# Spreading 1/rms over the partitions by GpSimd's DMAs, and the order of the last row block's tail, in a transformer layer on one core

## The chip, the cores and the metric

The kernel runs on one core of one Trainium2 chip. The metric is the device time in microseconds of one execution; lower is better. The kernel before took 351.38 us, the median of three runs (351.15 to 352.08).

## The reference, cut to what matters

x has 512 tokens of width 1024. Everything is float32, and the inputs are used once.

```python
def rmsnorm(x, g):
    y = x * lax.rsqrt(jnp.mean(x * x, axis=-1, keepdims=True) + 1e-6)
    return y * g

h = rmsnorm(x, g_mix)
q_sb, k_sb, v_sb, z_sb, q_mb, k_mb, v_mb, z_mb = split(h @ w_in, 8)     # 512 columns each
o_sb = stick_breaking_attention(q_sb, k_sb, v_sb)                       # 8 heads of 64
o_mb = moba_attention(q_mb, k_mb, v_mb, alibi_slopes)                   # 8 heads of 64
y = concat([rmsnorm(o_sb, g_out_sb) * silu(z_sb), rmsnorm(o_mb, g_out_mb) * silu(z_mb)])
x = x + y @ w_out
x = x + (p @ w_ple) * sigmoid(rmsnorm(x, g_ple) @ w_ple_gate)
out = rmsnorm(x, g_final)
```

The change touches two places: the first rmsnorm, whose 1/rms multiplies the projections q, k and z after the matmul, and the last rmsnorm, for the last 128 tokens.

## The kernel before, in words

**Matmuls in three parts.** Each float32 operand is split into a high and a low part (float32r): ScalarE writes the high part (`part_hi`, L80, the instruction at L82 or L84), VectorE subtracts it (`part_lo`, L86, the instruction at L88 or L90). `mul3` (L75) is then three matmuls of 128 x 128 by 128 x 512. Weights come as units of 512 KB (`load_unit`, L160, on SyncE's queue), wait in three buffers `raw`, and are split in the order of a list (`split_unit`, L197; `pop_w`, L105, takes one high part and the low part of the one before). When the low part of a unit's second half is done, the next unit is loaded.

**The opening.** The work is written out by hand in order for TensorE (always) and for ScalarE, VectorE and GpSimd (from L60 to L587). TensorE first does p @ w_ple (`ple`), then the projections of q0 and k0, then v0 (items of the list at L147). `stream` (L440) hands out these matmuls in steps of one `mul3`, and `F0(n)` (L446) takes n steps. v0 has four weight units; TensorE goes through them for the first two token blocks together, 4 steps a unit, 16 steps in all (L393 to L400), so the last unit is wanted from the thirteenth step on.

**1/rms of x.** VectorE and ScalarE sum the squares of x, tokens on partitions (`sq_x`, L487). `find_r` (L496) makes `r4` = (mean + eps)^-0.5 by a small VectorE instruction and GpSimd's power (`rstd`, L96, power at L99). r4 has 128 partitions x 4 token blocks. The projections q, k, z come out transposed (features on partitions, tokens along the row), so they need r4 along the row on every partition: `rx`, 128 x 512. `spread_r` (L501) makes it by four TensorE transposes of r4 broadcast over columns into one bank `tp`, and one ScalarE copy (L507). `scaled` (L295, VectorE at L298) multiplies a projection by rx into `ev`; `end_q` (L304) then copies parts of ev into QH (ScalarE, L313 and L314), subtracts into QL (VectorE, L315) and clears the other half of QL (GpSimd, L312); `end_k` (L317) does much the same. v needs r4 as it is.

In the order by hand, after `find_r` come the splits of two units of v0, eight steps of TensorE (last of q0, seven of k0), `spread_r`, one more step, three `pop_w` (L566; splits of v0's later units), `end_q0` (whose first VectorE instruction is ev), the remaining splits of v0, `end_k0`, and GpSimd's `rel` (iota and affine_select). Scores of the first head follow v0's first two token blocks.

**The rest.** Sixteen heads run as a pipeline: scores on TensorE, elementwise work on ScalarE and VectorE, transposes and the sums over v, with projection steps between them. Then come the output matmul, and per block of 128 tokens the gate: matmul, sigmoid, and the final norm.

**The tail.** The last token block (t = 3, from L952) does the gate in three cuts of 512, 256 and 256 columns (`gate_cut`, L963; `end_gate`, L911), sums squares per cut (`square_sum`, L970) and scales the two halves of the output. From L982 the order on ScalarE and VectorE is written by hand. `pre` gathers the mean of the first two cuts plus eps, `r3` is (sum + pre)^-0.5 by GpSimd's power (L990). The first half ot[0] was multiplied by g_final earlier and is scaled by ScalarE (L991); the second half ot[1] is multiplied by g_final on VectorE (L989) and then scaled by r3 (L992). The halves are stored from SyncE's queue (L993) and ScalarE's queue (L994).

Of the kernel before, what the change touches and what calls it, by code (L numbers as in the profile page):

```python
# [8 lines left out]
F32 = mybir.dt.float32  # L9
# [3 lines left out]
OP = mybir.AluOpType  # L13
ET = mybir.EngineType

P = 128
S = 512
# [6 lines left out]
NT = S // P  # L24
# [10 lines left out]
def layer(ctx, tc, x, xT, pT, w_qkz, w_v, gcols, g_final, w_out, w_ple, w_gate, out):  # L35
# [12 lines left out]
    nc = tc.nc  # L48
# [8 lines left out]
    dram = ctx.enter_context(tc.tile_pool(name="dram", bufs=1, space=bass.MemoryType.DRAM))  # L57
    pp = ctx.enter_context(tc.tile_pool(name="pp", bufs=1, space=bass.MemoryType.PSUM))
# [7 lines left out]
    def bank():  # L66
        return pp.tile([P, S], F32, name="pj", bufs=2)
# [4 lines left out]
    def tr(ps, src):  # L72
        nc.tensor.transpose(ps, src, idf)  # L73
# [6 lines left out]
    def part_hi(hi, src, scale=None):  # L80
        if scale is None:
            nc.scalar.copy(hi, src)  # L82
        else:
            nc.scalar.activation(hi, src, AF.Copy, scale=scale)  # L84

    def part_lo(hi, lo, src, scale=None):  # L86
        if scale is None:
            nc.vector.tensor_sub(lo, src, hi.bitcast(F32))  # L88
        else:
            nc.vector.scalar_tensor_tensor(lo, src, scale, hi.bitcast(F32), op0=OP.mult, op1=OP.subtract)  # L90
# [5 lines left out]
    def rstd(dst, ss, n, width):  # L96
        t = sm.tile([P, NT], F32, name="rs_t")
        nc.vector.tensor_scalar(t[:, :width], ss, 1.0 / n, EPS, op0=OP.mult, op1=OP.add)
        nc.gpsimd.tensor_tensor(dst, t[:, :width], mhalf[:, :width], op=OP.pow)  # L99
# [60 lines left out]
    def load_unit():  # L160
        if n_load[0] == len(UNITS):
            return
        kind, a, u = key = UNITS[n_load[0]]
        n_load[0] += 1
        r = raws[key] = raw.tile([P, DM], F32, name="raw")
        if kind == "v":
            load(r.rearrange("p (g c) -> p g c", g=2),
                 w_v[a:a + 2, u // 2, :, u % 2 * S:(u % 2 + 1) * S].rearrange("g p c -> p g c"))
        elif kind == "o":
            half, n = a  # L170
            row = (4 * half + 2 * u) * P
            load(r.rearrange("p (k c) -> p k c", k=2),
                 w_out[row:row + 2 * P, n * S:(n + 1) * S].rearrange("(k p) c -> p k c", p=P))
        elif kind == "g":
            load(r, w_gate[a * P:(a + 1) * P, :])
        else:
            load(r, w_qkz[12 * (a // 4) + BASE[kind] + a % 4])

    def gate_tiles(k):

        if k < 2:
            if k == 0:
                wg["big"] = big.tile([P, 2, 2, DM], F32R, name="wg01", tag="hTl")
            w = wg["big"][:, k]
        elif k == 2:
            w = at.tile([P, 2, DM], F32R, name="wg2", tag="v")
        elif k == 3:
            w = wu.tile([P, 2, DM], F32R, name="wg3", tag="wu")
        else:
            tags = {4: ("QH0", "QH1", "K0", "K1"), 5: ("QH0", "QH1", "K0", "K1"), 6: ("QL0", "QL1", "QL0", "QL1"),  # L190
                    7: ("y0", "y1", "y2", "y3")}[k]
            w = [(yp if g[0] == "y" else at).tile([P, S], F32R, name=f"wg{k}{i}", tag=g)
                 for i, g in enumerate(tags)]
            return [(w[n], w[2 + n]) for n in range(2)]
        return [(w[:, 0, n * S:(n + 1) * S], w[:, 1, n * S:(n + 1) * S]) for n in range(2)]

    def split_unit():  # L197

        if n_split[0] == len(UNITS):
            return  # L200
        kind, a, u = key = UNITS[n_split[0]]
        n_split[0] += 1
        parts = []
        scale = gc[:, 2 * KT + a:2 * KT + a + 1] if kind == "g" else None

        def hi_(n):
            if not parts:
                if kind == "g":
                    wg[a] = gate_tiles(a)
                    parts.extend(wg[a])  # L210
                else:
                    w = W_[key] = wu.tile([P, 2, DM], F32R, name="wu")
                    parts.extend((w[:, 0, n * S:(n + 1) * S], w[:, 1, n * S:(n + 1) * S]) for n in range(2))
            part_hi(parts[n][0], raws[key][:, n * S:(n + 1) * S], scale)

        def lo_(n):
            part_lo(*parts[n], raws[key][:, n * S:(n + 1) * S], scale)
            if n:
                whole.add(key)
                load_unit()  # L220

        wq.extend((lambda n=n: hi_(n), lambda n=n: lo_(n)) for n in range(2))
        if n_split[0] < len(UNITS) and UNITS[n_split[0]][0] == "g":
            split_unit()
# [76 lines left out]
    rx = {}  # L301
# [116 lines left out]
    x2 = [None]  # L418
# [27 lines left out]
    def F0(n):  # L446
        for _ in range(n):
            next(fs, None)
            steps[0] += 1
# [35 lines left out]
    ss4, r4 = (cst.tile([P, NT], F32, name=n) for n in ("ss4", "r4"))  # L485

    def sq_x(t):  # L487
        x_ = xs[t // 2][:, t % 2]
        if t % 2:
            nc.vector.tensor_tensor_reduce(out=x_, in0=x_, in1=x_, scale=1.0, scalar=0.0, op0=OP.mult, op1=OP.add,  # L490
                                           accum_out=ss4[:, t:t + 1])
        else:
            junk = at.tile([P, DM], BF16, name="junk", tag="o")
            nc.scalar.activation(junk, x_, AF.Square, accum_out=ss4[:, t:t + 1])

    def find_r():  # L496

        rstd(r4, ss4, DM, NT)
        rx["t"] = r4

    def spread_r():  # L501

        ps = pp.tile([P, S], F32, name="tp", bufs=2)
        for t in range(NT):
            tr(ps[:, t * P:(t + 1) * P], r4[:, t:t + 1].broadcast_to([P, P]))
        rx["all"] = yp.tile([P, S], F32, name="rx")
        nc.scalar.copy(rx["all"], ps)  # L507

    warm(28)
    nc.vector.tensor_copy(half((0, 0))[:, 0], rh[0, 0])  # L510
# [44 lines left out]
    for t in range(NT):  # L555
        sq_x(t)
    find_r()
    split_unit()
    split_unit()
    while wq or pend:  # L560
        pop_w()
    F0(8)
    spread_r()
    F0(1)
    end_q0, end_k0 = first
    for _ in range(3):  # L566
        pop_w()
# [196 lines left out]
    for h in range(2 * NH):  # L764
        if h == 0:
            front(0)
        else:
            b = h - 1
# [47 lines left out]
    b = 2 * NH - 1  # L816
# [17 lines left out]
    gf = at.tile([P, DM], F32, name="gf", tag="B", bufs=1)  # L834
# [73 lines left out]
                 k == 0, k == KT - 1)  # L908
            tick()

    def end_gate(t, a, b, ps, r, pt, between=None):  # L911
        gs = at.tile([P, S], F32, name="tmp")
        nc.scalar.activation(gs[:, :b - a], ps[:, :b - a], AF.Sigmoid, scale=r)
        nc.vector.tensor_mul(gs[:, :b - a], gs[:, :b - a], pt)  # L914
        if between:
            between()
        nc.vector.tensor_add(x2[0][:, t, a:b], x2[0][:, t, a:b], gs[:, :b - a])  # L917

    finish((0, 0))
# [12 lines left out]
    for t in range(NT - 1):  # L932
        r = rms2(t)
        pt = [at.tile([P, S], F32, name="pl", tag="ph", bufs=2) for n in range(2)]
        for n in range(2):
            load(pt[n], pl_d[t, :, n * S:(n + 1) * S])
        for n in range(2):
            ps = bank()
# [6 lines left out]
        r3 = rms2(t)  # L945
        for n in range(2):
            ns = slice(n * S, (n + 1) * S)
            ot = at.tile([P, S], F32, name="ot", tag="plo", bufs=2)
# [3 lines left out]
    t = NT - 1  # L952
    r = rms2(t)
    pt = [at.tile([P, S], F32, name="pl", tag="ph", bufs=2) for n in range(2)]
# [3 lines left out]
    ss = sm.tile([P, 3], F32, name="ss3")  # L958
    ot = [at.tile([P, S], F32, name="ot", tag="plo", bufs=2) for _ in range(2)]
    sq = at.tile([P, S], F32, name="sq", tag="o")  # L960
    pre, r3 = (sm.tile([P, 1], F32, name=n) for n in ("pre", "r3"))

    def gate_cut(c, between=None):  # L963
        a, b = cuts[c]
        ps = bank()
        gate_steps(t, ps, range(KT), a, b)
        end_gate(t, a, b, ps, r, pt[a // S][:, a % S:a % S + b - a], between)
        return x2[0][:, t, a:b]

    def square_sum(c):  # L970
        a, b = cuts[c]
        n, xc = b - a, x2[0][:, t, a:b]
        if c:
            nc.vector.tensor_tensor_reduce(out=sq[:, :n], in0=xc, in1=xc, scale=1.0, scalar=0.0,
                                           op0=OP.mult, op1=OP.add, accum_out=ss[:, c:c + 1])
        else:
            nc.scalar.activation(sq[:, :n], xc, AF.Square, accum_out=ss[:, :1])
# [4 lines left out]
    end = tc.manual_schedule(engines={ET.Activation, ET.DVE})  # L982
    end.__enter__()
    square_sum(1)
    gate_cut(2, between=lambda: nc.vector.tensor_add(pre, ss[:, 0:1], ss[:, 1:2]))
    nc.vector.tensor_scalar(pre, pre, 1.0 / DM, EPS, op0=OP.mult, op1=OP.add)
    square_sum(2)
    nc.vector.tensor_scalar(r3, ss[:, 2:3], 1.0 / DM, pre, op0=OP.mult, op1=OP.add)
    nc.vector.tensor_mul(ot[1], x2[0][:, t, S:], gf[:, S:])  # L989
    nc.gpsimd.tensor_tensor(r3, r3, mhalf[:, :1], op=OP.pow)  # L990
    nc.scalar.activation(ot[0], ot[0], AF.Copy, scale=r3)  # L991
    nc.vector.tensor_scalar_mul(ot[1], ot[1], r3)  # L992
    nc.sync.dma_start(out[t * P:, S:], ot[1])  # L993
    nc.scalar.dma_start(out[t * P:, :S], ot[0])  # L994
    end.__exit__(None, None, None)
# [32 lines left out]
```

## Time and profile before

| | |
|---|---|
| median of 3 runs | 351.38 us (351.15 to 352.08) |
| profiled execution | 352.3 us, span 350.5 us, granted TensorE clock 0.996 |
| busy: TensorE, its weight loads | 341.8 us (98%), 285.1 us (81%) |
| busy: VectorE, ScalarE, GpSimd | 279.6 us (80%), 220.6 us (63%), 19.6 us (6%) |
| DMA | 43.31 MB, from SyncE's queue but for the last store, on ScalarE's |

The span runs from the first to the last instruction. Engines work side by side, and a busy share is an average over all stages. In the rows below PE is TensorE's matmul, PEld its weight load, DVE VectorE, ACT ScalarE, POOL GpSimd, SP SyncE; a q behind an engine's name is its instruction queue. Times are in us.

### The profile page before, as it was taken

Reading aid. Unit: us, or ns where it says so; the run is one execution under the profiler, and the core shown is the slowest. Engines: PE = TensorE matmul, PEld = TensorE weight load, DVE = VectorE, ACT = ScalarE, POOL = GpSimd, SP = SyncE. Lnnn points to the kernel's source line nnn. Section 1 sums busy time; section 2 is a strip of 40 time slices with the busy share of each in tenths; the row PEclk is TensorE's granted clock in tenths of the full one; section 3 lists DMA queues with packets and bytes.
Section 4 is the critical chain, followed back from the end, with each engine's and each line's share of the span. In section 5 each row is a group of like instructions: output and inputs, shape, how many; then the busy total and the mean of one; then the engine's idle time right before and its main releaser. Section 6 shows DMA issues by size and latency. Waiting matters only on the chain.

```text
span 350.5 us, 4873 instructions
## 1 busy us (share of the span) xinstructions
PE 341.8 (98%) x1688; PEld 285.1 (81%) x1688; DVE 279.6 (80%) x570; ACT 220.6 (63%) x416; POOL 19.6 (6%) x43
## 2 busy tenths in 40 slices
PE   8999999999999999999999999999999999999991
PEld 6788888888888888888888888888888888888891
DVE  3996799878989897989579889989899979274554
ACT  4876767664767364777387689797776753234341
POOL 2013000000000000000000100000000010000111
PEclk9999999999999999999999999999999999999998
DMA  7997815212141114111105301310911680437321
GB/s 201 422 363 236 279 25 216 75 47 66 53 144 38 65 57 152 43 55 63 52 0 180 122 1 60 122 60 4 352 65 59 184 298 29 153 90 239 122 91 60
DMA packets 17624, 43.31 MB, mean 124 GB/s; under 512 B 1856, under 2 KB 3648, under 8 KB 17600
## 3 DMA queue, kind: packets, MB, share of 16 engines
q1 hardware_dynamic: 17456, 42.75, 35.3%
q8 instruction: 13, 0.21, 0.3%
q10 hardware_dynamic: 144, 0.26, 0.2%
q14 instruction: 11, 0.09, 0.1%
HBM read 37.24 MB, written 5.77 MB: 123 GB/s over the span
## 4 chain that ended last, share of the span: by engine, by line
PE 92%; issue 2%; DMA 2%; ACT 1%; DVE 1%; SPq 0%; POOL 0%; POOLq 0%; DVEq 0%; ACTq 0%
PE pj L70 67%; PE sc L70 9%; PE av L70 8%; PE tp L73 6%; PE tp L70 3%; DMA rawh<-in_pT_dram 2%; SPq L158 0%; ACT junk L864 0%; POOL r L99 0%; POOLq L1024 0%; DVE ot L949 0%; ACT ot L991 0%; DVE tmp L914 0%; DVE x L917 0%; DVE pu L88 0%
## 5 line engine op out<-in xcount | busy, mean ns | idle before, releaser
L70 PE MATMUL pj<-hTh,wu 128*128 128x512 f32 x384 | 134.5, 401 | 0.0
L70 PEld LDWEIGHTS pj<-hTh,wu 128*128 128x128 f32 x384 | 72.2, 188 | 13.0
L70 PE MATMUL pj<-hTl,wu 128*128 128x512 f32 x192 | 75.1, 391 | 0.0
L82 ACT CAST wu<-raw 128x512 fp32r<-128x512 f32 x80 | 46.7, 618 | 24.5 <-PE pj L70 21.0
L88 DVE TENSOR_TENSOR wu<-raw,wu 128x512 fp32r<-128x512 f32 x80 | 52.8, 684 | 2.8 <-ACT wu L82 2.6
L70 PE MATMUL pj<-wg,h 128*128 128x512 f32 (+1 forms) x216 | 44.8, 368 | 0.0
L70 PEld LDWEIGHTS pj<-wg,h 128*128 128x128 f32 x216 | 37.4, 188 | 7.4
L70 PEld LDWEIGHTS pj<-hTl,wu 128*128 128x128 f32 x192 | 36.3, 189 | 5.1
L88 DVE TENSOR_TENSOR plo<-tp,ph 128x512 fp32r<-128x512 f32 (+1 forms) x48 | 28.5, 593 | 6.4 <-ACT ph L82 6.1
L82 ACT CAST ph<-tp 128x512 fp32r<-128x512 f32 (+1 forms) x48 | 24.5, 511 | 13.3 <-PE tp L73 13.2
L70 PE MATMUL pj<-wu,yh 128*128 128x512 f32 x96 | 30.9, 403 | 0.0
L70 PE MATMUL pj<-wu,hTh 128*128 128x512 f32 x96 | 30.1, 395 | 0.0
L621 DVE TENSOR_TENSOR_SCAN inc<-A,own 128x512 f32<-128x512 f32 (+3 forms) x32 | 24.7, 809 | 5.4 <-ACT A L616 5.4
L73 PEld LDWEIGHTS tp<-idf,C 128*128 128x128 f32 x160 | 20.4, 140 | 6.1
L73 PE MATMUL tp<-idf,C 128*128 128x128 f32 x160 | 25.2, 272 | 0.0
L70 PE MATMUL sc<-K,QH 128*128 128x512 f32 (+1 forms) x64 | 19.8, 323 | 0.0
L70 PEld LDWEIGHTS pj<-wu,hTh 128*128 128x128 f32 x96 | 17.3, 188 | 3.1
L658 ACT ACTIVATE C<-A,nm 128x512 f32<-128x512 f32 (+3 forms) x32 | 17.8, 558 | 3.2 <-DVE nm L654 3.0
L70 PE MATMUL av<-ph,v 128*128 128x512 f32 (+1 forms) x64 | 19.7, 309 | 0.0
L298 DVE TENSOR_TENSOR ev<-pj,rx 128x512 f32<-128x512 f32 x24 | 16.4, 684 | 3.9 <-PE pj L70 3.8
L70 PE MATMUL av<-plo,v 128*128 128x512 f32 (+1 forms) x64 | 19.1, 324 | 0.0
L70 PE MATMUL sc<-K,QL 128*128 128x512 f32 (+1 forms) x64 | 19.0, 323 | 0.0
(140 smaller groups left out, 554.6 us busy)
## 6 DMA issues: line engine op xcount, KB each, us to landing
raw<-in_w_qkz_dram SPq DMA_DIRECT2D x24, 512.0 KB, 4.0
raw<-in_w_v_dram SPq DMA_DIRECT2D x8, 512.0 KB, 3.4
raw<-in_w_out_dram SPq DMA_DIRECT2D x8, 512.0 KB, 3.7
raw<-in_w_gate_dram SPq DMA_DIRECT2D x8, 512.0 KB, 3.5
xt<-in_xT_dram SPq DMA_DIRECT2D x4, 512.0 KB, 7.5
xs<-in_x_dram SPq DMA_DIRECT2D x4, 512.0 KB, 10.0
pl_d<-pt SPq DMA_DIRECT2D x8, 256.0 KB, 5.5
x<-in_x_dram SPq DMA_DIRECT2D x4, 512.0 KB, 7.1
```

The costliest lines, as they stand in the source:

```text
L70: nc.tensor.matmul(ps, lhsT=lhsT, rhs=rhs, start=start, stop=stop)
L73: nc.tensor.transpose(ps, src, idf)
L82: nc.scalar.copy(hi, src)
L88: nc.vector.tensor_sub(lo, src, hi.bitcast(F32))
L298: nc.vector.tensor_mul(t, ps, rx["all"])
L621: nc.vector.tensor_tensor_scan(inc[:, c:c + b - a][:, ::-1], keep[:, a:b][:, ::-1], own[:, S - (b - a):][:, ::-1], 0.0, op0=OP.mult, op1=O ...
L658: nc.scalar.activation(w[:, a:b], s[:, a:b], AF.Exp, scale=QKS, bias=nm[:, i:i + 1], accum_out=l[:, i:i + 1])
```

## The change

`spread_r` no longer uses TensorE and ScalarE. GpSimd issues a DMA of r4 into a DRAM tile `r_d` of 4 x 128, so that tokens lie in a row, and then a DMA that reads this row of 512 into each of the 128 partitions of rx. The call moves up, from behind the eight TensorE steps to right behind `find_r`; on GpSimd's queue the two DMAs stand between the power that makes r4 and the QL memsets, iota and affine_select.

In the tail, the two VectorE instructions that make `pre` move ahead of the last cut's gate. The multiply of ot[1] by g_final, which stood between the VectorE instruction that makes r3's base and GpSimd's power, goes; after the power one scalar_tensor_tensor scales by r3 and multiplies by g_final in one pass over the 512 columns.

```diff
     def spread_r():
 
-        ps = pp.tile([P, S], F32, name="tp", bufs=2)
-        for t in range(NT):
-            tr(ps[:, t * P:(t + 1) * P], r4[:, t:t + 1].broadcast_to([P, P]))
+        r_d = dram.tile([NT, P], F32, name="r_d")
+        nc.gpsimd.dma_start(r_d.rearrange("t p -> p t"), r4)
         rx["all"] = yp.tile([P, S], F32, name="rx")
-        nc.scalar.copy(rx["all"], ps)
+        nc.gpsimd.dma_start(rx["all"], r_d.rearrange("(o t) p -> o (t p)", o=1).broadcast_to([P, S]))
...
     find_r()
+    spread_r()
     split_unit()
     split_unit()
     while wq or pend:
         pop_w()
-    F0(8)
-    spread_r()
-    F0(1)
+    F0(9)
     end_q0, end_k0 = first
...
     square_sum(1)
-    gate_cut(2, between=lambda: nc.vector.tensor_add(pre, ss[:, 0:1], ss[:, 1:2]))
+    nc.vector.tensor_add(pre, ss[:, 0:1], ss[:, 1:2])
     nc.vector.tensor_scalar(pre, pre, 1.0 / DM, EPS, op0=OP.mult, op1=OP.add)
+    gate_cut(2)
     square_sum(2)
     nc.vector.tensor_scalar(r3, ss[:, 2:3], 1.0 / DM, pre, op0=OP.mult, op1=OP.add)
-    nc.vector.tensor_mul(ot[1], x2[0][:, t, S:], gf[:, S:])
     nc.gpsimd.tensor_tensor(r3, r3, mhalf[:, :1], op=OP.pow)
     nc.scalar.activation(ot[0], ot[0], AF.Copy, scale=r3)
-    nc.vector.tensor_scalar_mul(ot[1], ot[1], r3)
+    nc.vector.scalar_tensor_tensor(ot[1], x2[0][:, t, S:], r3, gf[:, S:], op0=OP.mult, op1=OP.mult)
```

## Rows read from the trace of the kernel before

**Rows 1.** The page's chain of work that ended last, by engine.

```profile
PE 92%; issue 2%; DMA 2%; ACT 1%; DVE 1%; SPq 0%; POOL 0%; POOLq 0%; DVEq 0%; ACTq 0%
```

**Rows 2.** Waits of TensorE: us in total, times, longest.

```profile
PE pj L70 <- POOL cold L276: 1.0, 1, 1.0
```

**Rows 3.** Timeline of TensorE: start, us, engine, line, operation, tiles, count.

```profile
27.32 0.39 PE L70 MATMUL pj<-hTh,wu 128*128 128x512 f32 x1
...
27.54 0.60 PE L73 MATMUL tp<-idf,r 128*128 128x128 f32 x4
...
28.68 0.62 PE L70 MATMUL av<-wu,hTh 128*128 128x512 f32 x2
...
36.85 0.62 PE L70 MATMUL av<-wu,hTh 128*128 128x512 f32 x2
```

**Rows 4.** Timeline of GpSimd, VectorE and ScalarE around rx.

```profile
24.74 1.03 POOL L99 TENSOR_TENSOR r<-rs_t,mhalf 128x4 f32<-128x4 f32 x1 [22.01 <-DVE rs_t L98]
...
25.11 2.61 DVE L88 TENSOR_TENSOR wu<-raw,wu 128x512 fp32r<-128x512 f32 x4 [0.46 <-ACT wu L82]
...
25.82 2.02 POOL L312 MEMSET QL<- 64x512 f32 x4
...
28.18 0.58 ACT L507 COPY rx<-tp 128x512 f32<-128x512 f32 x1 [1.27 <-PE tp L73]
...
30.53 0.68 DVE L298 TENSOR_TENSOR ev<-pj,rx 128x512 f32<-128x512 f32 x1
...
33.89 1.29 DVE L88 TENSOR_TENSOR wu<-raw,wu 128x512 fp32r<-128x512 f32 x2
```

**Rows 5.** DMA issues by line: count, KB each, median us to landing.

```profile
pl_d<-pt SPq DMA_DIRECT2D x8, 256.0 KB, 5.5
...
pl<-pl_d SPq DMA_DIRECT2D x8, 256.0 KB, 3.4
out_dram<-ot SPq DMA_DIRECT2D x7, 256.0 KB, 2.0
...
gc<-in_gcols_dram SPq DMA_DIRECT2D x1, 12.0 KB, 5.0
```

**Rows 6.** DMAs that write or read y_d, fifteen in all.

```profile
DMA to landing us min/median/max: 2.5/2.9/3.9
```

**Rows 7.** DMA queue of ScalarE, 346 to 350.6: packets, MB, share.

```profile
q10 hardware_dynamic: 144, 0.26, 14.8%
```

**Rows 8.** Timeline of the tail.

```profile
343.67 0.42 DVE L914 TENSOR_TENSOR tmp<-tmp,pl 128x256 f32<-128x256 f32 x1 [0.58 <-ACT tmp L913]
344.01 0.15 DVE L985 TENSOR_TENSOR pre<-ss 128x1 f32<-128x1 f32 x1
...
345.18 0.68 DVE L989 TENSOR_TENSOR ot<-x,gf 128x512 f32<-128x512 f32 x1
345.35 0.92 POOL L990 TENSOR_TENSOR r<-r,mhalf 128x1 f32<-128x1 f32 x1 [6.99 <-DVE r L988]
346.30 0.72 ACT L991 ACTIVATE ot<-ot,r 128x512 f32<-128x512 f32 x1 [2.66 <-POOL r L990]
346.30 0.49 DVE L992 TENSOR_SCALAR ot<-ot,r 128x512 f32<-128x512 f32 x1 [0.44 <-POOL r L990]
346.81 0.33 SPq L993 DMA_DIRECT2D out_dram<-ot  x1
347.05 0.37 ACTq L994 DMA_DIRECT2D out_dram<-ot  x1
```

**Rows 9.** Instructions of L99 and L949: duration ns minimum, median, maximum.

```profile
L99 POOL TENSOR_TENSOR r<-rs_t,mhalf x10: 538/546/1373, 24.7 to 337.8; 128x1 f32<-128x1 f32 x7, 128x4 f32<-128x4 f32 x3
...
L949 DVE SCALAR_TENSOR_TENSOR ot<-x,r,gf x6: 743/750/752, 314.0 to 336.9; 128x512 f32<-128x512 f32 x6
```

**Rows 10.** Stretches of the end: busy of each engine, clock, DMA share, GB/s.

```profile
347.75:348.00 0.25, 0.00 (x0) 0.00 (x0) 0.00 (x0) 0.00 (x0) 0.00 (x0) 0.50 1.09 418
...
348.75:349.00 0.25, 0.00 (x0) 0.00 (x0) 0.00 (x0) 0.00 (x0) 0.00 (x0) 0.50 0.90 344
```

More of the change, by code (lines that the diff above doesn't have):

```diff
@@ L909, in gate_steps, with end_gate @@
             tick()
-    def end_gate(t, a, b, ps, r, pt, between=None):
+    def end_gate(t, a, b, ps, r, pt):
         gs = at.tile([P, S], F32, name="tmp")
@@ L914, in end_gate @@
         nc.vector.tensor_mul(gs[:, :b - a], gs[:, :b - a], pt)
-        if between:
-            between()
         nc.vector.tensor_add(x2[0][:, t, a:b], x2[0][:, t, a:b], gs[:, :b - a])
@@ L961, in layer, with gate_cut @@
     pre, r3 = (sm.tile([P, 1], F32, name=n) for n in ("pre", "r3"))
-    def gate_cut(c, between=None):
+    def gate_cut(c):
         a, b = cuts[c]
@@ L966, in gate_cut @@
         gate_steps(t, ps, range(KT), a, b)
-        end_gate(t, a, b, ps, r, pt[a // S][:, a % S:a % S + b - a], between)
+        end_gate(t, a, b, ps, r, pt[a // S][:, a % S:a % S + b - a])
         return x2[0][:, t, a:b]
```

## The prediction

> **What bounds the kernel now.** I read the page first, then TensorE's waits, then the order of time around the two edited places, then the DMA issues. The chain of work that ended last is TensorE for 92% of the span [rows 1], and TensorE's own waits hold one row worth naming: 1.0 us, for the very first tile [rows 2]. So from the warm-up to the last gate matmul TensorE goes from one matmul to the next, and two kinds of change can move the time: fewer instructions on TensorE (or a stall put between them), and a shorter way from the last matmul to the last store. This change does one of each, and it puts something new in front of VectorE at the first.
>
> **Front: what goes.** The four transposes that spread r4 stand between matmuls of q0/k0. From 27.32 to 28.68 us TensorE issues four matmuls and four transposes [rows 3]. The cadence of such matmuls is (36.85 - 28.68) / 36 = 0.227 us (12 steps of 3) [rows 3], so the four matmuls alone take 0.91 and the transposes 1.36 - 0.91 = 0.45 us. With TensorE never waiting afterwards, that is 0.45 us off the end, if nothing new stalls it. ScalarE also loses its copy of 0.58 us [rows 4]; ScalarE is not on the path here, so I count nothing for it, except that the splits behind it come that much earlier.
>
> **Front: what comes.** r4 is written by GpSimd's power, 24.74 + 1.03 = 25.77; its next instruction began at 25.82 [rows 4]. From 25.82 two DMAs run one after the other: 2 KB out to DRAM as 512 pieces of four bytes (r4 lies with tokens on partitions, r_d is read along tokens), then 256 KB back, one row of 2 KB to each of 128 partitions. The second can't be issued before the first has landed, as it reads what that wrote. GpSimd stands in between: queued behind its second DMA are the QL memsets, iota and affine_select (four memsets take 2.02 [rows 4]), wanted by the first scores some ten microseconds later at the earliest, so that wait costs nothing by itself.
>
> The trace has no DMA issued by GpSimd and none in four-byte pieces, so both prices are bounds. Write: at least 2.0, the fastest landing in the kernel (output stores late in the kernel, when the queues are emptier); at most 5.0, gcols, the one transfer in small pieces (12 KB over 128 partitions), issued among the opening loads [rows 5]. Nearest in role is the later pair y_d/xb, which also goes to DRAM and back: 2.9 median to landing for either half [rows 6]. On top come the pieces: the last store's 144 packets held 14.8% of 16 engines for 4.6 us, 10.9 / 144 = 0.076 us each [rows 7]; if four bytes cost what 2 KB do, 512 / 16 x 0.076 = 2.4 us, if they cost by bytes, nothing. I take a third, 0.8: write 3.7. Read: at least 2.0, at most 5.5 (pl_d, the same 256 KB, stored in this very stretch); nearest is pl<-pl_d, the same 256 KB read back from DRAM, 3.4 [rows 5]; I take that. So rx is there at 25.82 + 3.7 + 3.4 = 32.92 us, bounds 25.82 + 4.0 = 29.82 and 25.82 + 10.5 = 36.32.
>
> The Trainium skill (DMA: Bandwidth & Descriptors, Anatomy of one DMA) puts a DMA issued from GpSimd at about 2.0 us fixed plus bytes / 436 GB/s; by that page the pair would take an estimated 2.0 + 2.6 = 4.6 us and rx would be in time. The same page (Rules for kernel authors) warns that a last dimension that isn't contiguous becomes one descriptor per element, which speaks against the write. No run shown here has such a DMA.
>
> **Front: when rx is too late.** VectorE works in the order written. Before, ev (q0 scaled by rx) began at 30.53, and 4.65 us later, at 33.89 + 1.29 = 35.18, VectorE ended the splits of v0's last weight unit [rows 4]: behind ev stand ScalarE's four QH copies, VectorE's two QL subtractions and then these splits, all in order on both engines. TensorE first needs that unit's low half one matmul after 36.85 [rows 3], at 37.08; with the transposes gone, at 36.63. So ev may begin as late as 36.63 - 4.65 = 31.98, and rx may land until about 31.9. The first score matmuls behind leave more room, as k0's end runs at the same distance from ev.
>
> At 32.92 rx is 1.02 us past it, and TensorE stalls so long. Sum of the front: -0.45 + 1.02 = +0.57, bounds -0.45 (any rx up to 31.9) and -0.45 + 4.42 = +3.97. What else hangs on ev, SP's loads of the next weights, goes to tiles that TensorE reaches only after two more v blocks; one microsecond is hidden there.
>
> **Tail.** pre's two instructions move ahead of the last cut, into the 0.58 us in which VectorE waits for ScalarE's sigmoid [rows 8]. They take 0.15 and about as much, so they fit; but where they stood they cost nothing either: L985 began 0.34 after L914, inside its 0.42 [rows 8]. So zero. The power (POOL L990) took 0.92 beside VectorE's multiply of two SBUF tiles (345.18 to 345.86) [rows 8]; the median of L99, seven of ten of that one column shape, is 0.546 [rows 9]. With VectorE at rest I take 0.55: end at 345.90 instead of 346.27. Then ScalarE's scaling, 0.72, and VectorE's pass, now a scalar_tensor_tensor as in L949, 0.75 instead of 0.49 [rows 8, 9]. Issues: 345.93 + 0.72 + 0.03 = 346.68 on ScalarE's queue (was 347.05) and 345.93 + 0.75 + 0.02 = 346.70 on SP's (was 346.81). The two stores share the DMA engines: from 347.75 on to 349 they move some 400 GB/s, near or at full share [rows 10]. So the end follows the first issue, 346.81 - 346.68 = 0.13 us sooner; if it followed the last, 347.05 - 346.70 = 0.35. I take 0.13, as the share is full throughout.
>
> The row of 0.92 shows the power ending 0.41 after the multiply. The Trainium skill (SBUF — State Buffer, two separate sides) says that a VectorE instruction with two SBUF inputs and a GpSimd one that reads SBUF exclude each other for the whole instruction; by that rule the power would end 0.55 after 345.86, at 346.41, 0.14 later than measured, and the gain of resting would be 0.5 instead of 0.37. The trace agrees in kind, not fully in size, and the sum goes by the trace.
>
> **Sum.** +0.57 - 0.13 = +0.44 us. The profiled execution took 352.3 us (span 350.5 and 1.8 around it), so 352.74; it lies 0.92 above the median of the runs, 351.38, and I put the difference on that: 351.8.
>
> **Rivals.**
> A. rx comes in time (write and read together at most 6.1 us). For: two bare landings of 2.0 or the y_d/xb pair at 2 x 2.9 = 5.8 would do it [rows 5, 6]. Against: that pair moves long runs, and pl_d, stored from the same stretch on, took 5.5 [rows 5]. Time: -0.45 - 0.13 = -0.58, 350.8.
> B. The round trip becomes the bound, slower than before: the place is VectorE's ev, behind which ScalarE's copies and the last v0 split stand; the price is one for one, each microsecond of rx behind 31.9 is one of TensorE. It decides "slower" from rx = 31.9 + 0.58 + 1.05 = 33.5, a pair of 7.7 us. For: gcols' 5.0 and pl_d's 5.5, together 10.5 [rows 5]. Against: both rows were queued behind other transfers of SP's own queue, and GpSimd has its own. Time at the upper bound: 4.42 - 0.58 = +3.84, 355.2; half way to it from 33.5, near 353.8. One way into it would be that GpSimd can't make its descriptors while VectorE works on two SBUF tiles (until 25.11 + 2.61 = 27.72): 1.9 us more, 353.7. Against that: GpSimd's four memsets, which also write SBUF, ran beside those splits at 0.5 each [rows 4].
> C. The power doesn't shorten. Then VectorE's longer pass makes both issues 347.05 and 347.07, 0.24 after the old first one; the sum is +0.57 + 0.24 = +0.8, 352.2. Against: L99's median [rows 9].
> D. A gain above 0.3%. The terms allow at most 0.45 + 0.35 = 0.8 us; no row gives more.
>
> **Chances.** Forecast (rx between 31.9 and 33.5, with C inside it) 0.37; A 0.24; B 0.34; D 0.05. 0.3% is 1.05 us, about what a measurement of this kernel can tell from no change (its three runs span 0.93). A and the forecast lie within it, so faster 0.05, same 0.61, slower 0.34. The range reaches from A with a little of the runs' spread, 350.6, to B with a pair of some 9.3 us, 354.0; I leave 0.15 above and below it together. The forecast's own range is 350.8 to 352.4.
>
> **What would show it.** GpSimd's two issues and the landing of rx: right if 32 to 33.5. ev's idle time on VectorE, released by the DMA of rx, and a new wait of TensorE on the splits of v0's last unit at about 36.4: its length is rx minus 31.9; none means A, over 1.6 means B. No tp<-idf,r in TensorE's rows at 27.5. In the tail the power at 0.55 and both issues within 0.05 us of each other; 0.9 means C. The forecast is wrong if rx lands outside 31.9 to 33.5, or if the wait falls on something behind ev that I gave room: the first scores, or weights of the next projections.

## The result and the profile after

The changed kernel takes 365.61 us (median of 6 runs, 363.59 to 367.15), the kernel before 351.35 us (6 runs, 350.86 to 353.61). The ratio is 1.0387 (95% interval 1.0344 to 1.043; the quotient of the two medians, 1.0406, lies inside it): 14.3 us slower by the medians, where 0.4 us was forecast and 354.0 was the upper end of the range.

TensorE's waits come first here, as in [rows 2]: which engine and line, for whom, us in total, times, longest. The kernel is the changed one.

```profile
PE av L70 <- ACT wu L82: 10.9, 1, 10.9
PE pj L70 <- POOL cold L276: 1.0, 1, 1.0
```

There is one new wait, of 10.9 us, for a split of v0's last weight unit. That is rival B's place. GpSimd's timeline of the changed kernel shows what is late (it answers to [rows 4]):

```profile
25.40 1.43 POOL L99 TENSOR_TENSOR r<-rs_t,mhalf 128x4 f32<-128x4 f32 x1 [22.66 <-DVE rs_t L98]
27.14 0.94 POOL L504 DMA_DIRECT2D r_d<-r  x1 [0.31 <-POOL r L99]
38.66 0.57 POOL L506 DMA_DIRECT2D rx<-r_d  x1 [10.58 <-DMA r_d<-r]
39.27 2.02 POOL L312 MEMSET QL<- 64x512 f32 x4
```

GpSimd issues the write of r4 into DRAM at 27.14, waits 10.58 us for it, and issues the read into rx at 38.66. The DMA issues of the changed kernel (count, KB, median us to landing; they answer to [rows 5]):

```profile
pl_d<-pt SPq DMA_DIRECT2D x8, 256.0 KB, 8.5
...
rx<-r_d POOLq DMA_DIRECT2D x1, 256.0 KB, 5.7
...
r_d<-r POOLq DMA_DIRECT2D x1, 2.0 KB, 11.2
```

Two kilobytes take 11.2 us to land, twice as long as the 256 KB read back, and pl_d's stores land later than before (8.5 against 5.5). VectorE and TensorE around it, from their timelines in the changed kernel (they answer to [rows 3, 4]):

```profile
44.40 0.69 DVE L298 TENSOR_TENSOR ev<-pj,rx 128x512 f32<-128x512 f32 x1 [15.45 <-DMA rx<-r_d]
...
47.77 1.29 DVE L88 TENSOR_TENSOR wu<-raw,wu 128x512 fp32r<-128x512 f32 x2
```

```profile
29.12 0.61 PE L70 MATMUL av<-wu,hTh 128*128 128x512 f32 x2
...
37.06 0.39 PE L70 MATMUL tp<-wu,hTl 128*128 128x512 f32 x1
48.34 1.57 PE L70 MATMUL av<-wu,hTh 128*128 128x512 f32 x2 [10.89 <-ACT wu L82]
...
49.12 0.29 PEld L70 LDWEIGHTS av<-wu,hTh 128*128 128x128 f32 x1 [0.49 <-DVE wu L88]
...
55.49 0.63 PE L70 MATMUL pj<-wu,hTh 128*128 128x512 f32 x2
```

VectorE stands idle for 15.45 us ahead of ev. The splits behind it end at 47.77 + 1.29 = 49.06, 4.66 us after ev began; 4.65 was read from before. TensorE goes on at 48.34, when ScalarE's last high part is there, and its second matmul waits 0.49 us more, for the low part that VectorE makes. Then the matmuls follow each other, but slowly. Stretches of the changed kernel (columns as in [rows 10], the last three are granted clock, DMA share and GB/s):

```profile
39.00:41.00 2.00, 0.00 (x0) 0.00 (x0) 0.00 (x0) 0.00 (x0) 1.91 (x5) 0.96 1.03 405
41.00:48.00 7.00, 0.00 (x0) 0.00 (x0) 2.30 (x4) 2.80 (x5) 1.41 (x3) 0.50 0.29 115
48.00:54.00 6.00, 5.66 (x13) 4.11 (x14) 4.80 (x9) 3.13 (x6) 0.00 (x0) 0.50 0.65 210
54.00:55.00 1.00, 1.00 (x5) 0.85 (x4) 0.41 (x3) 0.79 (x2) 0.00 (x0) 0.75 0.71 191
```

While TensorE stands, the granted clock falls to half (1.2 GHz), and it stays there for six microseconds of matmuls afterwards (0.50 from 48 to 54). The tail, the changed kernel's timeline (answers to [rows 8]):

```profile
360.10 0.54 POOL L986 TENSOR_TENSOR r<-r,mhalf 128x1 f32<-128x1 f32 x1 [6.71 <-DVE r L985]
360.67 0.72 ACT L987 ACTIVATE ot<-ot,r 128x512 f32<-128x512 f32 x1 [2.34 <-POOL r L986]
360.68 0.75 DVE L988 SCALAR_TENSOR_TENSOR ot<-x,r,gf 128x512 f32<-128x512 f32 x1 [0.66 <-POOL r L986]
361.43 0.40 ACTq L990 DMA_DIRECT2D out_dram<-ot  x1
361.45 0.33 SPq L989 DMA_DIRECT2D out_dram<-ot  x1
```

The tail does what was forecast: a power of 0.54 us, two issues 0.02 us apart.

### The profile page after: what moved, and what is told of

It reads as the page before. It is cut to its first block, busy times and chain, and to the rows that moved or that the text cites. A ratio compares the mean times of both kernels' runs of the same rounds, so it can differ in the third digit from the quotient of the medians.

```text
span 365.3 us, 4867 instructions
## 1 busy us (share of the span) xinstructions
PE 345.8 (95%) x1684; PEld 287.8 (79%) x1684; DVE 279.2 (76%) x569; ACT 220.1 (60%) x415; POOL 21.1 (6%) x45
## 4 chain that ended last, share of the span: by engine, by line
PE 78%; DMA 8%; DVE 6%; issue 3%; ACT 2%; POOL 1%; SPq 0%; POOLq 0%; DVEq 0%; ACTq 0%
PE pj L70 59%; PE sc L70 7%; PE av L70 6%; PE tp L73 5%; DMA r_d<-r 3%; DMA raw<-in_w_gate_dram 2%; PE tp L70 2%; DMA rx<-r_d 2%; DVE x L422 1%; POOL r L99 1%; DMA rawh<-in_pT_dram 1%; DVE wg L90 1%; DVE wu L88 1%; DVE xs L490 1%; ACT wu L82 0%
## 5 line engine op out<-in xcount | busy, mean ns | idle before, releaser
L82 ACT CAST ph<-tp 128x512 fp32r<-128x512 f32 (+1 forms) x48 | 24.5, 511 | 13.3 <-PE tp L73 13.1
L313 ACT CAST QH<-ev 64x512 fp32r<-64x512 f32 x16 | 9.9, 618 | 16.0 <-DVE ev L298 15.9
```

The costliest lines, as they stand in the source:

```text
L313: nc.scalar.copy(Qh[e][own_], ps[own_])
```

## Experiments

The questions were which of the two edits loses the time, why 2 KB need 11 us, and what the wait costs beyond its own length.

**The two halves of the change.** `tail_only` has the front of the kernel before and the changed tail, `front_only` the reverse.

```diff
# tail_only, against the changed kernel
     find_r()
-    spread_r()
...
-    F0(9)
+    F0(8)
+    spread_r()          # the transposes of before
+    F0(1)
```

> The front of the kernel before (transposes), with only the tail's edits. Theory: the power falls from 0.92 to 0.55 us, and as the two last stores share the DMA engines, the end comes some 0.13 us sooner (ratio 0.9996, not to be told from no change). Rival 1, the end follows the later of the two issues: 0.35 us (ratio 0.999). Rival 2, the tail's edits are a part of the 14 us lost: several us slower.

> The tail of the kernel before, with only the front's edits (1/rms spread by GpSimd's two DMAs). Theory: the whole loss is here, 14.2 to 14.6 us more than before (365.5 to 366), with the write landing after some 11 us and the read after some 5.7. Rival: part of the loss is in the tail, then less than 14.

Measured: `tail_only` 351.18 us (12 runs) against 351.24 (17 runs), ratio 0.9991 (0.9981 to 1.0001); `front_only` 364.55 us, ratio 1.0376 (1.0355 to 1.0397), with the write landing after 10.7 us and the read after 6.3. So the loss is the front's, 13.3 of the 14.3 us by the medians and within the intervals all of it; the time itself lies a microsecond below the 365.5 to 366 that I expected. The tail is no loss; whether it gains 0.1 or 0.35 us the interval doesn't tell. It is the only version here that may be better than the kernel before.

**Fewer and larger pieces.** `write16` writes r4 as it lies.

```diff
-        r_d = dram.tile([NT, P], F32, name="r_d")
-        nc.gpsimd.dma_start(r_d.rearrange("t p -> p t"), r4)
+        r_d = dram.tile([P, NT], F32, name="r_d")
+        nc.gpsimd.dma_start(r_d, r4)
```

> As the changed kernel, but r4 is written as it lies, 16 contiguous bytes from each of 128 partitions, instead of 512 pieces of four bytes; the row read back holds the same 512 values in another order, so q, k and z are scaled with the wrong tokens' values. Theory, the pieces make the write slow: a quarter of the pieces, so the write lands after 2 to 5 us instead of 11.2, rx comes 6 to 9 us sooner, and the time falls to 354 to 359. Rival 1, a DMA of GpSimd's queue is slow whatever it moves: the write lands after 9 us or more and the time stays at 363 or above. Rival 2, the transfers of SP's queue in the same stretch hold it up: likewise 9 us or more.

Measured: 358.92 us (4 runs), ratio 1.0215 (1.0188 to 1.0243); the write lands after 5.3 us, a little above the expected range, and TensorE waits 5.9. Same queue, same bytes, same stretch, half the landing time: rivals 1 and 2 fall as whole explanations. The four-byte pieces matter; whether by their number or otherwise this run doesn't say.

**Another queue.** `act_write` issues the same four-byte pieces from ScalarE's queue.

```diff
-        nc.gpsimd.dma_start(r_d.rearrange("t p -> p t"), r4)
+        nc.scalar.dma_start(r_d.rearrange("t p -> p t"), r4)
```

> As the changed kernel, but the write of r4 into DRAM, still 512 pieces of four bytes, is issued from ScalarE's queue; the read stays on GpSimd's. Theory, the pieces are slow whoever issues them: landing after 10 to 11.5 us, time 363 to 366. Rival, GpSimd's way of issuing is the slow part: landing after 2 to 5 us, time 354 to 359.

Measured: 366.18 us, ratio 1.0416 (1.0375 to 1.0458); landing after 11.6 us. Both lie a little above the theory's ranges and far from the rival's: who issues is not the matter.

**The write by itself, first try.** `bench` adds six DMAs to the kernel before, of the form that the next diff shows.

> The kernel before, with six more DMAs that nobody reads, each behind another head's start, where the DMA engines are mostly idle: 512 pieces of four bytes from GpSimd (b_4x512), 128 of 16 bytes (b_16x128), 512 of four bytes that lie 512 bytes apart in DRAM (b_apart), 128 of four bytes (b_4x128), 512 of four bytes from SyncE's queue (b_sp), and 128 rows of 2 KB from GpSimd (b_rows). Theory, each small piece costs: b_4x512 lands after 8 to 11 us, b_16x128 and b_4x128 after 3 to 5, b_sp about as b_4x512, b_rows after 2 to 3. Rival 1, GpSimd's queue: all of GpSimd's land after 8 us or more and b_sp after 2 to 4. Rival 2, contention in the opening: all land after 2 to 4. Rival 3, neighbouring pieces in the same stretch of DRAM get in each other's way: b_apart lands after 2 to 5 and b_4x512 after 8 or more.

Measured: 357.98 us in one run. This run failed as a measurement of prices: the five from GpSimd have nothing to wait for and were issued between 27.8 and 31.4 us, all in flight together, landing after 7.6 to 16.8 us. Two things it does show. The one from SyncE was issued alone, at 48.1, and landed after 11.5 us. And in this run the DMAs that nobody reads cost 6.7 us (against 351.24 for the kernel before in the same set): TensorE waits 4.0 us further on for a ScalarE instruction.

**The write by itself, one at a time.** `bench2` and `bench3` keep GpSimd in written order behind instructions that wait for the heads. They took 351.47 and 351.31 us, one run each.

```diff
+        if h == 2:
+            d = dram.tile([NT, P], F32, name="b_4x512")
+            nc.gpsimd.dma_start(d.rearrange("t p -> p t"), r4)
...
+        elif h == 6:
+            d = dram.tile([NT, P, 128], F32, name="b_apart")
+            nc.gpsimd.dma_start(d.rearrange("t p w -> p t w")[:, :, :1], r4.rearrange("p (t w) -> p t w", w=1))
```

> The kernel before, with GpSimd kept in written order and seven more DMAs that nobody reads, each behind another head's start, so that no two of them run together: from GpSimd 512 pieces of four bytes (b_4x512), 128 of 16 bytes (b_16x128), 512 of four bytes that lie 512 bytes apart in DRAM (b_apart), 128 of four bytes (b_4x128), 128 rows of 2 KB stored (b_rows) and one row of 2 KB read into 128 partitions (at the last head, over rx, which is done by then); from SyncE 512 of four bytes (b_sp). Theory, each small piece written costs: b_4x512 and b_sp land after 8 to 11.5 us, b_16x128 and b_4x128 after 3 to 5.5, the rows and the read after 2 to 3.5. Rival 1, the busy DMA engines of the opening made it slow: b_4x512 and b_sp land after 2 to 5. Rival 2, neighbouring pieces in the same stretch of DRAM get in each other's way: b_apart after 2 to 5, b_4x512 after 8 or more.

> The kernel before, GpSimd in written order, with five more DMAs that nobody reads, one at a time in stretches with little DMA traffic: 512 pieces of four bytes side by side (b_next), 64 bytes apart (b_sixtyfour), 32 bytes apart (b_thirtytwo), all from GpSimd; at the end GpSimd reads 128 different rows of 2 KB into rx (from w_out), and then SyncE reads one row of 2 KB into all 128 partitions. Theory (neighbours): b_next lands after 7 to 11 us, b_sixtyfour after 2 to 5, b_thirtytwo between or as one of them; and for the read, one row read 128 times is what is slow: the different rows land after 2 to 3.5 us, the one row from SyncE after 5 to 7.5. Rivals: b_next at 2 to 4 (then it was the busy opening); both reads alike (then it is GpSimd's queue or the size).

DMA issues of `bench2` (the name's digits behind an x are left out; the first b_4x is 512 pieces, the second 128):

```profile
b_rows<-rx POOLq DMA_DIRECT2D x1, 256.0 KB, 2.3
rx<-in_g_final_dram POOLq DMA_DIRECT2D x1, 256.0 KB, 7.2
...
b_4x<-r POOLq DMA_DIRECT2D x1, 2.0 KB, 10.7
b_16x<-r POOLq DMA_DIRECT2D x1, 2.0 KB, 2.8
b_apart<-r POOLq DMA_DIRECT2D x1, 2.0 KB, 2.2
b_4x<-r POOLq DMA_DIRECT2D x1, 0.5 KB, 7.3
b_sp<-r4b SPq DMA_DIRECT2D x1, 2.0 KB, 8.2
```

DMA issues of `bench3`:

```profile
rx<-in_w_out_dram POOLq DMA_DIRECT2D x1, 256.0 KB, 7.4
rx<-in_g_final_dram SPq DMA_DIRECT2D x1, 256.0 KB, 3.6
b_next<-r POOLq DMA_DIRECT2D x1, 2.0 KB, 11.4
b_sixtyfour<-r POOLq DMA_DIRECT2D x1, 2.0 KB, 2.2
b_thirtytwo<-r POOLq DMA_DIRECT2D x1, 2.0 KB, 3.6
```

My theory up to here, a price per small piece, falls: 512 pieces of four bytes land after 2.2 us when they lie 512 or 64 bytes apart in DRAM, after 3.6 us at 32 bytes, and after 8.2 to 11.4 us side by side; 128 pieces side by side (7.3) are slower than 512 apart. The rival that neighbours get in each other's way holds. It holds outside the opening too: b_next was issued at 54.8 us, and b_sp at 202.7, to land at 210.9. For half of b_sp's time the profile shows the DMA engines idle (columns as in [rows 10]):

```profile
204.00:208.00 4.00, 4.00 (x23) 3.44 (x22) 3.33 (x10) 3.97 (x11) 0.00 (x0) 1.00 0.00 0
```

So neither other transfers nor busy engines account for that part of the 8.2 us. Some things stay open. b_apart and b_sixtyfour had almost no other traffic beside them, b_thirtytwo and b_next had weight loads, so 3.6 against 2.2 may be the loads and not the distance. Pieces further apart are also spread over more of DRAM, and no run separates the two. And 128 pieces of 16 bytes, side by side, landed after 2.8 us: touching alone isn't what is slow.

The reading half of the test decided nothing: the 7.2 and 7.4 fell into a stretch in which the engines were full (share 0.97 from 245 to 249 us in `bench2`), and there one row and 128 different rows cost alike; one row from SyncE at 252.1 took 3.6. So one row read 128 times isn't what is slow, against my expectation of the reverse.

**In place, with nobody waiting.** `unread` is the kernel before plus the write alone, right behind r4; `unread_apart` has its pieces 512 bytes apart.

```diff
     find_r()
+    r_d = dram.tile([NT, P], F32, name="r_d")          # [NT, P, 128], first of 128, in unread_apart
+    nc.gpsimd.dma_start(r_d.rearrange("t p -> p t"), r4)
     split_unit()
```

> The kernel before, transposes and all, with one DMA more right behind r4: GpSimd writes r4 into DRAM as the changed kernel does, 512 pieces of four bytes side by side, and nobody reads it. Theory now, pieces of four bytes next to each other in DRAM are slow and hold up whatever runs on the DMA engines beside them: the write lands after 9 to 11.5 us, and pl_d's stores and the weight loads beside it land after 8 or more; as nothing on TensorE's path waits for them in time, 0 to 2 us slower than before (351.3 to 353.3). Rival, it is only slow because the waiting kernel stands still: landing after 2 to 5.

> The same as the run above with the 512 pieces of four bytes 512 bytes apart in DRAM. Theory (neighbours in the same stretch of DRAM get in each other's way): lands after 2 to 4 us in the same busy stretch, pl_d stays at some 5.5, and the time is that of before within 0.3%. Rival (the count of pieces, with the engines busy): lands after 9 us or more, as the run above.

Measured: `unread` 351.88 us (10 runs, 351.17 to 357.23), ratio 1.0012 (0.9997 to 1.0027) without the two longest of the ten; `unread_apart` 351.40 us (10 runs, 350.99 to 352.45), ratio 1.0 (0.9987 to 1.0013). DMA issues from 24 to 40 us, first of `unread`, then of `unread_apart`:

```profile
raw<-in_w_qkz_dram SPq DMA_DIRECT2D x3, 512.0 KB, 10.8
pl_d<-pt SPq DMA_DIRECT2D x6, 256.0 KB, 11.2
raw<-in_w_v_dram SPq DMA_DIRECT2D x1, 512.0 KB, 3.3
r_d<-r POOLq DMA_DIRECT2D x1, 2.0 KB, 11.1
```

```profile
raw<-in_w_qkz_dram SPq DMA_DIRECT2D x4, 512.0 KB, 4.9
pl_d<-pt SPq DMA_DIRECT2D x7, 256.0 KB, 5.6
raw<-in_w_v_dram SPq DMA_DIRECT2D x1, 512.0 KB, 3.4
r_d<-r POOLq DMA_DIRECT2D x1, 2.0 KB, 4.0
```

Same place, same queue, same count of pieces: 11.1 against 4.0 us, and only the neighbouring ones hold up transfers beside them (q, k and z weights 10.8 against 4.9, pl_d 11.2 against 5.6; the load of v's weights, issued 0.4 us behind the write, is not held up, 3.3 against 3.4). This pair is the clean test, as the place and the traffic are the same in both. By itself the write is hidden in eight executions of ten; two, at 356.9 and 357.2, took 5 us more, and why stays open.

**The price of the wait.** `busy` and `busy2` put idle matmuls into the place where TensorE waits.

```diff
-    F(8)
+    F(4)
+    sc3 = pp.tile([P, 3 * S], F32, name="sc")
+    for _ in range(44):                       # 55 in busy2
+        mm(sc3[:, :S], hT[0][:, 0, :P], hT[0][:, 0, :], True, True)
+    F(4)
```

> As the changed kernel, with 44 matmuls that nobody reads put on TensorE ahead of v0's last weight unit (about 44 x 0.227 = 10.0 us at the full clock), in the place where it waits 10.9 us. Theory: the loss of 14.3 us is the wait of 10.9 plus about 3 us in which TensorE goes on at half its granted clock afterwards; with work in the wait the clock stays at 1.0, and the kernel gets about 3 us faster though TensorE does more: 362 to 363. Rival, the clock costs nothing, the rest of the loss is elsewhere: 365 or more.

> As the run before with idle work in TensorE's wait, now with 55 matmuls that nobody reads (12.5 us) instead of 44, so that no rest of the wait is left. Theory: the granted clock stays at 1.0 throughout and the kernel is 2.5 to 3 us faster than the changed one, 362.3 to 363.3. Rival, the low clock costs only what the run with 44 gave back: 364 or more.

Measured: `busy` 364.20 us (4 runs, 363.52 to 364.98), `busy2` 364.47 (4 runs, 363.55 to 365.35), against 365.61 (363.59 to 367.15) for the changed kernel. Both expectations were missed; 364.47 lies where the rival of `busy2` put it, and the three medians can't be told apart by their intervals (ratios 1.0338 to 1.0384, 1.034 to 1.0404 and 1.0344 to 1.043). In `busy` the matmuls ended too early: a wait of 1.9 us was left, and the clock fell all the same, though only after TensorE had gone on (0.50 from about 48.3 to 51.6 us):

```profile
47.28 0.50 PE L70 MATMUL av<-wu,hTh 128*128 128x512 f32 x1 [1.94 <-ACT wu L82]
```

```profile
47.00:48.00 1.00, 0.50 (x1) 0.19 (x1) 1.00 (x3) 0.23 (x1) 0.00 (x0) 1.00 0.00 0
...
49.00:50.00 1.00, 1.00 (x4) 0.81 (x3) 0.69 (x1) 0.95 (x3) 0.00 (x0) 0.50 0.92 262
```

In `busy2` nothing was left to wait and the clock stayed at 1.00, but the write landed after 8.7 us there, VectorE's last split was done at 46.01 + 1.29 = 47.30, and the idle matmuls went on until 49.95: they had become the bound themselves. The first matmul behind the scores is 13.1 us later than before (53.95 against 40.84), which is the whole of the loss (364.47 against 351.37). So the rival's number came for another reason than its own, and the time of this run doesn't decide what the clock costs. What the low clock costs can be read without the medians. TensorE's timeline of `busy2` over the same instructions as above, from v0's last unit to the first matmul behind the scores; ahead of it VectorE's last split:

```profile
46.01 1.29 DVE L88 TENSOR_TENSOR wu<-raw,wu 128x512 fp32r<-128x512 f32 x2
```

```profile
49.95 0.62 PE L70 MATMUL av<-wu,hTh 128*128 128x512 f32 x2
...
53.95 0.63 PE L70 MATMUL pj<-wu,hTh 128*128 128x512 f32 x2
```

At the full clock they take 53.95 - 49.95 = 4.00 us, in the changed kernel 55.49 - 48.34 = 7.15. A part of this, 0.5 us, is the low half of the split, for which the second matmul still waits; the rest, about 2.6 us, is the clock. That low clock and a wait go together is shown (behind 10.9 and 1.9 us, and not in `busy2`); as a saving in the whole kernel's time it isn't, since the idle matmuls fill the time they save.

## Why the prediction was wrong, point by point

**The bound of the write was the step that failed.** "Write: at least 2.0 ...; at most 5.0, gcols, the one transfer in small pieces", and "I take a third, 0.8: write 3.7". Measured 11.2. gcols reads DRAM in pieces of 96 bytes (12 KB over 128 partitions); r_d is written in pieces of four, side by side. I scaled by the number of pieces and used a price per packet of 2 KB rows, so that even the worst case (2.4 us on top) had no place for what the runs show: the same number of pieces of the same size costs 2.2 us at 64 bytes' distance and 11.4 without. No row of before shows a write of this kind, and the bound should have been left open upwards instead of closed by a row of another kind. With it the range's upper end, 354.0, was too low, and rival B's upper price, 355.2. A row was misread besides: 2.9 is the median of y_d's and xb's DMAs together, not of either half; by line the stores take 3.6 us and the reads 2.8, a pair of 6.4, so this support of rival A lay above A's own limit of 6.1.

The estimate by the Trainium skill's page (DMA: Bandwidth & Descriptors, Anatomy of one DMA; 2.0 + 2.6 = 4.6 us for the pair) was further off than the rows: 11.2 + 5.7 = 16.9 measured. The Trainium skill's warning (the same page, Rules for kernel authors), one descriptor per element, names the right suspect, but `b_apart`, cut into the same 512 elements, lands after 2.2 us. The Trainium skill (DMA: Bandwidth & Descriptors, Specifications) also says that below 512 bytes the engine reads, modifies and writes; pieces of four bytes at 64 bytes' distance do so as well by that rule, so the trace shows that this alone isn't slow. That it becomes slow where several pieces meet in one stretch of DRAM fits these runs; why it does, they don't show.

**The read** was put at 3.4 and took 5.7. From 39 to 41 us the engines are full (1.03, 405 GB/s) with pl_d's stores and weights that the slow write had held back and that now run beside it. That they are held back isn't needed for it: in `write16`, where pl_d lands after 5.5 as before, the read still takes 5.3. That full engines are the cause is argued from the rows; no run isolates it.

**When rx is there.** Forecast 32.92; it landed at 44.31. The difference of 11.4 is 7.5 from the write, 2.3 from the read, 1.1 from a later end of r4's power (26.83 for 25.77), and 0.5 for two gaps of 0.3 us ahead of GpSimd's issues, of which I had counted 0.05.

**What a late rx costs.** "One for one" from 31.9 on gives 44.31 - 31.9 = 12.4 us. TensorE reached the place 0.9 us later in this execution than the sum assumed (its opening ran late; `front_only`'s did not), which leaves 11.5; the waits are 10.9 and 0.5. So the mechanism, the place and the distance of 4.65 us were right. What was missing is the clock: 2.6 us that no term of the sum had, though the trace before shows the fall to half in its last microseconds, when TensorE has nothing left to do [rows 10].

**The sum, again.** 0.9 later at the place, less the 0.45 us of the transposes, is the 0.44 us by which v0 begins later (29.12 against 28.68); waits 11.4; clock 2.6. Together 14.4 of the 14.65 us by which the first matmul behind the scores is late (55.49 against 40.84, from TensorE's timeline before):

```profile
40.84 0.63 PE L70 MATMUL pj<-wu,hTh 128*128 128x512 f32 x2
```

The transposes' 0.45 us were rightly priced; nothing was gained by saving them.

**The tail was right.** The power fell from 0.92 to 0.54, the pass took 0.75, and the first store's issue came 1.33 us after the power began instead of 1.46. The last bytes moved 3.58 us after the power's start instead of 3.68: 0.10 us gained where 0.13 was forecast. The chip's runs can't tell that from nothing (0.9991, 0.9981 to 1.0001).

**The rivals.** B came, far beyond its upper price. Its variant, descriptors held up by VectorE's splits, did not: GpSimd's issue of the write took 0.94 us and ended at 28.08, while VectorE's splits ran on to 28.95, and the write from ScalarE's queue is as slow. C did not come.

## What to carry to other kernels

Before a value goes through DRAM to change its layout, look at which side breaks it into pieces and whether these pieces lie next to each other in DRAM: 512 four-byte writes side by side took 8.2 to 11.6 us here and held up most transfers beside them; 16-byte pieces took 2.8 to 5.3, and four-byte pieces 64 or 512 bytes apart 2.2 to 4.0. Set four TensorE transposes (0.45 us) against a round trip through DRAM only after the trip's slowest plausible landing has been compared with the slack behind the waiting instruction; here even 2.2 + 3.6 us, with a gap of 0.3 ahead of each issue, would have brought rx at 25.77 + 6.4 = 32.2, 0.3 us too late. Price a wait of several microseconds on TensorE with matmuls at half the clock behind it (2.6 us here). And where the trace has no operation of a kind, its upper bound is open, whatever the nearest row says.

## What the runs showed that I had not expected

512 four-byte pieces written 64 bytes apart land as fast (2.2 us) as 256 KB stored in rows of 2 KB (2.3 us), while the same pieces side by side take 11.4 us and, in `unread`, bring another queue's 512 KB loads from 4.9 to 10.8 us. TensorE's clock fell in `busy` behind a rest of only 1.9 us, with matmuls at the full clock right before the rest, and stayed low from about 48.3 to 51.6 us, three microseconds of work.

GpSimd's power for r4 took 1.43 us in the changed kernel and 1.03 before. In the first VectorE's subtraction of two SBUF tiles had begun before it (25.25 against 25.40), in the second after it (25.11 against 24.74). The other runs go the same way: 1.46 in `write16` and 1.43 in `busy2`, with VectorE first, 1.03 in `unread`, with GpSimd first. That it is the same meeting as in the tail, where resting VectorE gave 0.38 us back, fits all of these; no run was made for it.
